# A hybrid attention/RWKV block on one core: key norm at written places, and a reordered end

## The chip, the cores and the metric

The kernel runs on one core of a Trainium2 chip. The metric is the device time of one execution in microseconds (us), as the median of several runs; lower is better. The core has five engines with queues of their own: PE multiplies matrices, DVE and ACT work elementwise (ACT evaluates functions such as Ln and Exp, for which it loads tables), POOL (GpSimd) is a slower elementwise engine, and SP issues most DMAs. Each engine takes its instructions in order; between engines they wait on semaphores.

## The reference

One layer of a trunk with a sequence of 256 tokens and a width of 2048, in float32. A normed input goes through one combined projection; three mixers (stick-breaking attention, forgetting attention, RWKV-7 time mixing) work on it; gated, projected and normed it is added to the input, and a squared-ReLU MLP follows, normed and added as well:

```python
u = rms_norm(x, norm_mix_pre)
proj = u @ w_in
m = g_a * (y_a @ w_branch_a) + g_b * (y_b @ w_branch_b) + g_c * (y_c @ w_branch_c)
x = x + rms_norm(m @ w_out, norm_mix_post)
hdn = square(relu(rms_norm(x, norm_mlp_pre) @ w_mlp_up))
x = x + rms_norm(hdn @ w_mlp_down, norm_mlp_post)
```

In the RWKV part a key vector of each of 16 heads (64 wide) is normed at each token, and a state is carried over the sequence:

```python
kk = kk / maximum(sqrt(sum(kk * kk, axis=-1, keepdims=True)), 1e-12)
sa = einsum('bhvk,bhk->bhv', state, kk_t)
state = state * w_t - sa * (kk_t * a_t) + v_t * k_t      # outer products
y_t = einsum('bhvk,bhk->bhv', state, r_t)
```

## The kernel before, in words

**Matrix products.** All big products run on PE in a split form: a float32 weight chunk of 128x1024 (`raw`) comes by DMA from SP, ACT copies it to a rounded high part `whi` (L152), DVE forms the rest `wlo` (L153), and PE multiplies both with the split activations, adding into the PSUM tiles `gps` (L168, L172 for products with channels on the partitions; L198, L214 for those with tokens there). Three buffers each of `raw`, `whi` and `wlo` rotate, and one chunk is prepared ahead. This stream goes through the whole kernel.

**Mixers beside the stream.** The mixers are Python generators. While the GEMMs are recorded, a model clock advances with each matmul, and a generator is resumed when its due time has come (`yield 3.8`) or when what it names is there (`yield "k3"`). So its small instructions land between the GEMM's in each engine's queue. PE's order in this part is the recorded one (`manual_schedule`); on the other engines a scheduler decides, unless an instruction is pinned with `pin`, which keeps it at its recorded place in its engine's queue.

**The RWKV halves.** `rwkv_half(hf)` handles 8 heads in four pairs `p`, in four chunks of 64 tokens. Each chunk `c` is a chain over the engines: PE adds the state's part (L869, from the state `PB`), ACT and DVE copy it out as `rh` (L873, L874), PE multiplies it with the chunk's triangular inverse (L842 and L882, interleaved), ACT and DVE copy the result into the two tiles `XT` (L886, L887, in turns), PE forms the state's update and the output (L894, L898, L903), DVE updates `PB` (L912, L913 or L915), and ACT copies the output into `g` tiles (L917). After the fourth chunk `gate_norm` starts (L944 to L978, tiles `gn`; its sums are PE's L954).

**Key norm.** `key_norm(hf)` computes the inverse norms of the keys of a half in the tile `b` (by its tag `b6`): four squares on ACT (L635), a split into high (ACT, L646) and low (DVE, L647) of two pairs at a time, sums over a head by PE with a block matrix of ones (L653), a floor (DVE, L655, `sq`), Ln and Exp on ACT with a table load ahead of each (L659, L662), and a Newton step on DVE of five operations a pair of pairs (L667 to L672). `key_norm(0)` runs ahead of the first half's chain. `key_norm(1)`, for the second half, is started as a generator of its own after the first half's first chunk, so that its steps fall beside the chain of the other chunks; the second half reads it much later.

**The end.** The last product (hidden times `w_mlp_down`, the part that is not done in a Strassen-like form above it) goes over four groups `g` of 512 output columns. For each group and token tile `tt` (two of 128 tokens), DVE adds PE's sum to `y` (L1540), ACT squares it with a row sum (L1541), and DVE multiplies it with the gain (L1544). In the last group PE finishes tile 0 first, then tile 1. For each, `rs` comes from DVE (L1139) and a power on POOL (L1140); four final pieces of 512 columns follow on DVE (L1555), each with a store from SP (L1556).

Of the kernel before, what the change touches and what calls it, by code (L numbers as in the profile page):

```python
# [10 lines left out]
F32 = mybir.dt.float32  # L11
F32R = mybir.dt.float32r
# [38 lines left out]
def hybrid_block(ctx, tc, xt, x, gains, params, consts, lora, gup, wst, out):  # L51
# [13 lines left out]
    def nm(s):  # L65
        uid[0] += 1
        return f"{s}_{uid[0]}"
# [4 lines left out]
    def mps():  # L72
        return pm.tile([128, 512], F32, tag="mps", name=nm("mps"), bufs=4)
# [17 lines left out]
    def P(name, i=0, r=slice(0, 128)):  # L91
        return par[r, PC[name] + i:PC[name] + i + 1]
# [535 lines left out]

    def key_norm(hf):
        PR = range(4 * hf, 4 * hf + 4)  # L630
        B6 = rp.tile([128, 6, T], F32, tag="b6", name=nm("b6"), bufs=1)
        rin = [B6[:, i, :] for i in range(4)]
        for i, p in enumerate(PR):
            yield f"k{p}"
            A.activation(rin[i], done[f"k{p}"], AF.Square, scale=P("kk", p))  # L635
        sq = []
        for both in ((0, 1),) if hf == 0 else ((0,), (1,)):
            sqh = []
            for i2 in both:
                s = B6[:, 2 * i2:2 * i2 + 2, :]  # L640
                if hf == 0:
                    hl = [rp.tile([128, 2, T], F32R, tag="BK", name=nm("sqh"), bufs=8) for _ in range(2)]
                else:
                    t = rp.tile([128, 4, T], F32R, tag="Ti", name=nm("sqh"), bufs=1)
                    hl = [t[:, 0:2], t[:, 2:4]]
                A.activation(hl[0], s, AF.Copy)  # L646
                V.tensor_tensor(hl[1], s, hl[0].bitcast(F32), ALU.subtract)  # L647
                sqh.append(hl)
            yield 3.8
            for hl in sqh:  # L650
                ps = mps()
                for n, part in enumerate(hl):
                    PE.matmul(ps.rearrange("p (a b) -> p a b", a=2), bones, part, start=n == 0, stop=n == 1)  # L653
                sq.append(rp.tile([128, 2, T], F32, tag="At", name=nm("sq"), bufs=2))
                V.tensor_scalar(sq[-1], ps.rearrange("p (a b) -> p a b", a=2), 1e-24, None, ALU.max)  # L655
        if hf:
            yield 2.0
        for i2 in range(2):
            A.activation(B6[:, 2 * i2:2 * i2 + 2, :], sq[i2], AF.Ln, scale=float(2.0 ** 20))  # L659
        for i2 in range(2):  # L660
            ri = B6[:, 2 * i2:2 * i2 + 2, :]
            A.activation(ri, ri, AF.Exp, scale=-0.5)  # L662
        yield 4.5
        sc = B6[:, 4:6, :]
        for i2 in range(2):
            ri = B6[:, 2 * i2:2 * i2 + 2, :]
            V.tensor_scalar(ri, ri, 1024.0, None, ALU.mult)  # L667
            V.tensor_tensor(sc, ri, ri, ALU.mult)
            yield 2.0
            V.tensor_tensor(sc, sc, sq[i2], ALU.mult)  # L670
            V.tensor_scalar(sc, sc, -0.5, 1.5, ALU.mult, ALU.add)
            V.tensor_tensor(ri, ri, sc, ALU.mult)  # L672
            yield 3.0
        kin[hf] = rin
        mark(f"kn{hf}")

    def rwkv_half(hf):
# [184 lines left out]
        def duo(ps, hc, d):  # L862
            return ps[hc, 128 * d:128 * d + 128].rearrange("p (a b) -> p a b", a=2)

        for c in range(4):
            if c:
                for i, p in enumerate(PR):
# [17 lines left out]
            for d in range(2):  # L885
                A.activation(XT[d][0:64, :, c, HC[0]], duo(ps, HC[0], d), AF.Copy)  # L886
                V.tensor_copy(XT[d][0:64, :, c, HC[1]], duo(ps, HC[1], d))  # L887
            yield 2.2
            ps = mps()
            psp, psy = ps[:, 0:256], ps[:, 256:512]  # L890
# [9 lines left out]
            if c:  # L900
                for i, p in enumerate(PR):
                    for h, hc in enumerate(HC):
                        PE.matmul(psy[hc, 64 * i:64 * i + 64], PB[:, i, hc], Bt[p][:, c, 64:128], start=False,  # L903
                                  stop=i == 3)
# [624 lines left out]
    for g in range(4):  # L1529
# [7 lines left out]
                    nc.sync.dma_start(out=x1[tt][:, c:c + 1024], in_=xs[tt][:, c:c + 1024])  # L1537
        for tt, ps in enumerate(tok(hp, 3 if g == 3 else 1)):
            yv = ys[tt][:, gs]
            V.tensor_tensor(yv, yv, ps, ALU.add)  # L1540
            A.activation(junk(), yv, AF.Square, accum_out=ss4[:, tt, g:g + 1])  # L1541

            def gained():
                V.tensor_tensor(yv, yv, g4[g], ALU.mult)  # L1544

            if g < 3:
                gained()
                if g == 2:
                    sum4.append(rstd_of(ss4[:, tt, :], eps4[tt], None))
            else:  # L1550
                r4 = rstd_of(ss4[:, tt, :], None, sum4[tt])
                gained()
                for c in range(0, D, 512):
                    cs = slice(c, c + 512)
                    V.scalar_tensor_tensor(x1[tt][:, cs], ys[tt][:, cs], r4, x1[tt][:, cs], ALU.mult, ALU.add)  # L1555
                    nc.sync.dma_start(out=out[tt * 128:tt * 128 + 128, cs], in_=x1[tt][:, cs])  # L1556


# [123 lines left out]
```

## Time and profile before

| what | us |
|---|---|
| median of three runs (lowest, highest) | 1505.39 (1505.01, 1508.8) |
| profiled execution, its own time | 1504.03 |
| its span, first to last instruction | 1502.3 |
| PE busy in the span | 1482.0 |
| DVE busy | 1215.5 |
| ACT busy | 938.5 |
| POOL busy | 91.3 |

Times inside the program are read from the one profiled execution, on a scale that begins with its first instruction. The second to fourth chunk of the first half run from about 408 to 442 us on it, and the end begins at about 1487. A line number is that of the kernel before. In the trace's timeline a row has the start, the length, the engine, the line, the operation, the tiles (out<-in), the shape and how many such instructions in a row it merges; in square brackets stands how long the engine had been idle before it, and what released it.

### The profile page before, as it was taken

To read this page: it belongs to the slowest core of one execution; us is meant where nothing else is said; L and a number is where in the kernel's file an instruction comes from. 1 tells how busy PE (TensorE), PEld (TensorE's weight loads), DVE (VectorE), ACT (ScalarE), POOL (GpSimd) and SP (SyncE) were. 2 spreads that over 40 slices of the span, in tenths; PEclk is the share of its full clock that TensorE was granted. 3 is DMA by queue.
4 is the path that set the end of the run, shared out by engine and by line. 5 is a ranking of instruction groups with operands and counts; after the bars stand their busy time and mean duration, and the time that the engine had idled before them with its cause. 6 is when DMAs were issued, how large, how long until landed. Compare 5 with 4: busy or idle time off the path is not lost.

```text
span 1502.3 us, 22802 instructions
## 1 busy us (share of the span) xinstructions
PE 1482.0 (99%) x8401; PEld 1249.1 (83%) x8401; DVE 1215.5 (81%) x1687; ACT 938.5 (62%) x1398; POOL 91.3 (6%) x160
## 2 busy tenths in 40 slices
PE   9999999999999999999999999999999999999997
PEld 7888888888778888788887888888888888888885
DVE  7666677999769898567646788999899999899986
ACT  7465666664667554575444767777667676677662
POOL 0021000100001100000000000000000000000000
PEclk9999999999999999999999999999999999999998
DMA  7545545545535455445774668888888888888874
GB/s 258 196 150 188 174 169 170 178 164 193 187 116 181 160 181 199 153 147 197 264 281 169 223 207 241 266 241 246 259 263 251 264 255 228 252 259 272 257 247 152
DMA packets 107615, 317.70 MB, mean 211 GB/s; under 512 B 10736, under 2 KB 14704, under 8 KB 107248
## 3 DMA queue, kind: packets, MB, share of 16 engines
q1 hardware_dynamic: 94832, 284.91, 54.9%
q0 software_dynamic: 8064, 29.36, 10.4%
q10 hardware_dynamic: 4608, 1.97, 0.5%
q8 instruction: 66, 1.08, 0.3%
q14 instruction: 45, 0.37, 0.1%
HBM read 282.65 MB, written 4.19 MB: 191 GB/s over the span
## 4 chain that ended last, share of the span: by engine, by line
PE 69%; DVE 1%; issue 1%; POOL 0%; POOLq 0%; ACT 0%; DVEq 0%; ACTq 0%
PE gps L214 20%; PE gps L168 15%; PE gps L172 8%; PE gps L198 5%; PE mps L1412 3%; PE mps L1413 3%; PE mps L1414 3%; PE gps L1414 3%; PE gps L1412 2%; PE gps L1413 2%; PE gps L176 1%; PE mps L767 0%; PE mps L976 0%; DVE wlo L153 0%; PE mps L1103 0%
## 5 line engine op out<-in xcount | busy, mean ns | idle before, releaser
L153 DVE TENSOR_TENSOR wlo<-raw,whi 128x1024 fp32r<-128x1024 f32 x501 | 608.3, 1223 | 162.7 <-ACT whi L152 147.8
L152 ACT ACTIVATE whi<-raw 128x1024 fp32r<-128x1024 f32 x501 | 527.7, 1057 | 260.3 <-PE gps L214 94.1
L168 PE MATMUL gps<-pk,whi 128*128 128x512 f32 x1366 | 346.4, 393 | 0.6 <-ACT whi L152 0.4
L168 PEld LDWEIGHTS gps<-pk,whi 128*128 128x128 f32 x1366 | 253.0, 189 | 50.5 <-ACT whi L152 0.6
L214 PE MATMUL gps<-whi,pk 128*128 128x512 f32 x1144 | 288.5, 392 | 0.0
L214 PEld LDWEIGHTS gps<-whi,pk 128*128 128x128 f32 x1144 | 212.8, 188 | 44.3
L172 PEld LDWEIGHTS gps<-pk,wlo 128*128 128x128 f32 x1456 | 198.5, 190 | 14.4 <-DVE wlo L153 0.5
L172 PE MATMUL gps<-pk,wlo 128*128 128x256 f32 x1456 | 204.1, 282 | 0.0
L214 PE MATMUL gps<-wlo,pk 128*128 128x512 f32 x572 | 156.4, 392 | 0.0
L214 PEld LDWEIGHTS gps<-wlo,pk 128*128 128x128 f32 x572 | 106.3, 188 | 22.4 <-DVE wlo L153 0.3
L1304 ACT ACTIVATE sp<-gps 128x512 f32<-128x512 f32 x52 | 31.1, 598 | 86.2 <-PE gps L176 86.0
L1278 DVE TENSOR_TENSOR sp<-raw,sp 128x1024 fp32r<-128x1024 f32 x67 | 82.0, 1224 | 3.4 <-ACT sp L1277 3.1
L1277 ACT ACTIVATE sp<-raw 128x1024 fp32r<-128x1024 f32 x67 | 70.6, 1054 | 12.8 <-PE mps L1413 4.9
L198 PE MATMUL gps<-whi,pk 128*128 128x512 f32 x264 | 71.0, 391 | 0.0
L1412 PE MATMUL mps<-whi,fm 128*128 128x512 f32 x168 | 66.2, 394 | 0.0
L1413 PE MATMUL mps<-whi,fm 128*128 128x512 f32 x168 | 65.8, 392 | 0.0
L1414 PE MATMUL mps<-wlo,fm 128*128 128x512 f32 x168 | 65.5, 390 | 0.0
L1374 POOL DMA_DIRECT2D raw<-raw x40 | 35.0, 874 | 427.6 <-DVE wlo L153 106.0
L198 PEld LDWEIGHTS gps<-whi,pk 128*128 128x128 f32 x264 | 49.2, 188 | 10.4 <-ACT whi L152 0.2
L1414 PE MATMUL gps<-wlo,fm 128*128 128x512 f32 x126 | 49.2, 391 | 0.5 <-DVE wlo L153 0.5
L1371 DVE TENSOR_TENSOR raw<-raw,raw 128x1024 f32<-128x1024 f32 x40 | 48.9, 1223 | 0.4
L1412 PE MATMUL gps<-whi,fm 128*128 128x512 f32 x126 | 49.2, 391 | 0.0
(378 smaller groups left out, 1962.3 us busy)
## 6 DMA issues: line engine op xcount, KB each, us to landing
raw<-in_wst_dram SPq DMA_DIRECT2D x499, 512.0 KB, 4.3
raw<-raw POOLq DMA_DIRECT2D x40, 512.0 KB, 6.4
sp<-in_wst_dram SPq DMA_DIRECT2D x16, 512.0 KB, 5.3
raw<-sp POOLq DMA_DIRECT2D x8, 512.0 KB, 6.1
sp<-raw POOLq DMA_DIRECT2D x8, 512.0 KB, 6.6
x<-in_x_dram SPq DMA_DIRECT2D x8, 256.0 KB, 5.9
xs<-x SPq DMA_DIRECT2D x2, 1024.0 KB, 3.9
x<-xs SPq DMA_DIRECT2D x4, 512.0 KB, 6.0
```

Source lines behind the costliest of these rows:

```text
L152: A.activation(hi, raw, AF.Copy)
L153: V.tensor_tensor(lo, raw, hi.bitcast(F32), ALU.subtract)
L168: PE.matmul(ps, hi[:, i * 128:i * 128 + 128], pks[i], start=first and i == 0, stop=False)
L172: PE.matmul(ps[:, 0:T], lo[:, i * 128:i * 128 + 128], pks[i][:, 0:T], start=False, stop=False)
L198: PE.matmul(ps[tt], pks[k][:, c:c + 128], w[:, (k - k0) * 512:(k - k0) * 512 + 512], start=k == 0 and part == 0 and w is hl[0], stop=w is ...
L214: PE.matmul(ps[tt], pks[k][:, c:c + 128], w[:, (k - k0) * 512:(k - k0) * 512 + 512], start=k == 0 and part == 0 and w is hl[0], stop=False)
L1277: A.activation(hi, raw, AF.Copy)
L1278: V.tensor_tensor(lo, raw, hi.bitcast(F32), ALU.subtract)
L1371: V.tensor_tensor(x, x, z, ALU.add)
L1412: PE.matmul(Q[f], p, w, start=d == 0 and i == 0, stop=False)
L1413: PE.matmul(Q[f], pl, w, start=False, stop=False)
L1414: PE.matmul(Q[f], p, wl, start=False, stop=d == nd - 1 and i == 1)
```

## The change

The change has two parts. The first is about key norm of the second half. Its generator is no longer started on its own; the first half's chunk loop resumes it at fixed places (`next(beside, None)`): after the XT copies of a chunk and at the end of a chunk. Its yields lose their times, its ACT instructions and the Newton step are pinned, its two Ln stand together and its two Exp, and the Newton step comes behind the fourth chunk. The second part is about the end: the second tile's sum is put ahead of the last two final pieces of the first tile (`issue_after`), one final piece of the second tile is made by ACT (scaling) and GpSimd (adding) and stored from ACT's queue, and the last piece and its store are halved.

```diff
     def key_norm(hf):
+        keep = pin if hf else lambda ins: ins
...
+        def high_low(i2):
...
+            keep(A.activation(hl[0], s, AF.Copy))
+            keep(V.tensor_tensor(hl[1], s, hl[0].bitcast(F32), ALU.subtract))
+            return hl
+
+        def summed(hl):
+            ps = mps()
+            for n, part in enumerate(hl):
+                PE.matmul(ps.rearrange("p (a b) -> p a b", a=2), bones, part, start=n == 0, stop=n == 1)
+            sq.append(rp.tile([128, 2, T], F32, tag="At", name=nm("sq"), bufs=2))
+            V.tensor_scalar(sq[-1], ps.rearrange("p (a b) -> p a b", a=2), 1e-24, None, ALU.max)
...
-        for both in ((0, 1),) if hf == 0 else ((0,), (1,)):
...
+        else:
+            hl = high_low(0)
+            yield
+            summed(hl)
+            hl = high_low(1)
+            yield
+            summed(hl)
+            yield
+        for i2 in range(2):
+            keep(A.activation(B6[:, 2 * i2:2 * i2 + 2, :], sq[i2], AF.Ln, scale=float(2.0 ** 20)))
         if hf:
-            yield 2.0
+            yield
         for i2 in range(2):
             ri = B6[:, 2 * i2:2 * i2 + 2, :]
-            A.activation(ri, ri, AF.Exp, scale=-0.5)
+            keep(A.activation(ri, ri, AF.Exp, scale=-0.5))
         yield 4.5
...
+        beside = iter(()) if hf else key_norm(1)
         for c in range(4):
...
+            if c:
+                next(beside, None)
             yield 2.2
...
-            if c == 0 and hf == 0:
-                start(key_norm(1))
...
+            next(beside, None)
             yield 2.6
+        for _ in beside:
+            pass
         start(gate_norm(hf, y, bon))
...
-            V.tensor_tensor(yv, yv, ps, ALU.add)
+            added = V.tensor_tensor(yv, yv, ps, ALU.add)
...
+            if tt == 0:
+                r4 = rstd_of(ss4[:, 0, :], None, sum4[0])
+                gained()
+                final(0, 512)
+                final(512, 512)
+                r40 = r4
+                continue
+            with tc.issue_after(added.ins):
+                for c in (1024, 1536):
                     cs = slice(c, c + 512)
+                    V.scalar_tensor_tensor(x1[0][:, cs], ys[0][:, cs], r40, x1[0][:, cs], ALU.mult, ALU.add)
+                    nc.sync.dma_start(out=out[0:128, cs], in_=x1[0][:, cs])
+            r4 = rstd_of(ss4[:, 1, :], None, sum4[1])
+            gained()
+            t, cs = junk(), slice(0, 512)
+            A.activation(t, ys[1][:, cs], AF.Copy, scale=r4)
+            G.tensor_tensor(x1[1][:, cs], x1[1][:, cs], t, ALU.add)
+            nc.scalar.dma_start(out=out[128:256, cs], in_=x1[1][:, cs])
+            for c, w in ((512, 512), (1024, 512), (1536, 256), (1792, 256)):
+                final(c, w)
```

The line numbers of the changed kernel are higher by some 15 to 20 from key norm on. Its order at three places follows. First ACT's queue from the third chunk's `rh` copy (L873, in the changed kernel L890) to the split in front of the fourth chunk's: `b` is key norm's tile, `sq` its sums, `XT` the chain's copies, `whi` a weight split, `g` the output copies. Before:

```order
L873 ACTIVATE rh_4330<-mps_4233 64x128 x2
L662 ACT_TABLE_LOAD
L662 ACTIVATE b_773_4166<-b_773_4166 128x512
L152 ACTIVATE whi_4435<-raw_4433 128x1024
L886 ACTIVATE XT_3445<-mps_4357 64x2x64
L886 ACTIVATE XT_3446<-mps_4357 64x2x64
L152 ACTIVATE whi_4469<-raw_4467 128x1024
```

And in the changed kernel:

```order
L890 ACTIVATE rh_4330<-mps_4225 64x128 x2
L152 ACTIVATE whi_4433<-raw_4431 128x1024
L903 ACTIVATE XT_3445<-mps_4353 64x2x64
L903 ACTIVATE XT_3446<-mps_4353 64x2x64
L672 ACT_TABLE_LOAD
L672 ACTIVATE b_773_4166<-sq_4251 128x512
L672 ACTIVATE b_773_4166<-sq_4302 128x512
L152 ACTIVATE whi_4464<-raw_4462 128x1024
L934 ACTIVATE g_754_4073<-mps_4392 128x64
```

The two XT copies stand ahead of the table load, and both Ln come behind them; the second load and the two Exp follow behind the `g` copies, ahead of the fourth chunk's `rh`.

Then DVE's queue at the first half's fourth chunk, from its second XT copy on, where `gn` is the gate norm, `gup` a small weight of it and `wlo` a weight split. Before:

```order
L887 COPY XT_3446<-mps_4479 64x2x64
L153 TENSOR_TENSOR wlo_4585<-raw_4582,whi_4584 128x1024
L948 TENSOR_TENSOR gn_4556<-gn_4557,gn_4555 128x512
L937 TENSOR_TENSOR gup_4645<-gup_4562,gup_4645 128x128
L938 TENSOR_TENSOR gup_4645<-gup_4562,gup_4645 32x128
```

And in the changed kernel:

```order
L904 COPY XT_3446<-mps_4474 64x2x64
L682 TENSOR_SCALAR b_773_4166<-b_773_4166 128x512
L683 TENSOR_TENSOR b_773_4166<-b_773_4166 128x512
L686 TENSOR_TENSOR b_773_4166<-b_773_4166,sq_4251 128x512
L687 TENSOR_SCALAR b_773_4166<-b_773_4166 128x512
L688 TENSOR_TENSOR b_773_4166<-b_773_4166 128x512
L683 TENSOR_TENSOR b_773_4166<-b_773_4166 128x512
L968 TENSOR_TENSOR gn_4556<-gn_4557,gn_4555 128x512
L686 TENSOR_TENSOR b_773_4166<-b_773_4166,sq_4302 128x512
L153 TENSOR_TENSOR wlo_4585<-raw_4582,whi_4584 128x1024
```

Nearly the whole Newton step now lies behind the last XT copy and among the first instructions of the gate norm.

Last, DVE's queue at the end of the program, from the first tile's power on; `x` is the tile of final pieces (2583 the first, 2584 the second). Before:

```order
L1555 SCALAR_TENSOR_TENSOR x_2583_14109<-y_8767,rs_14256,x_2583_14109 128x512 x4
L1540 TENSOR_TENSOR y_8768<-y_8768,gps_14204 128x512
L1139 TENSOR_SCALAR rs_14289<-ss_8074,ssum_14200 128x1
L1544 TENSOR_TENSOR y_8768<-y_8768,pk_13934 128x512
L1555 SCALAR_TENSOR_TENSOR x_2584_14110<-y_8768,rs_14289,x_2584_14110 128x512 x4
```

And in the changed kernel:

```order
L1574 SCALAR_TENSOR_TENSOR x_2583_14109<-y_8767,rs_14256,x_2583_14109 128x512 x2
L1560 TENSOR_TENSOR y_8768<-y_8768,gps_14204 128x512
L1587 SCALAR_TENSOR_TENSOR x_2583_14109<-y_8767,rs_14256,x_2583_14109 128x512 x2
L1159 TENSOR_SCALAR rs_14289<-ss_8074,ssum_14200 128x1
L1564 TENSOR_TENSOR y_8768<-y_8768,pk_13934 128x512
L1574 SCALAR_TENSOR_TENSOR x_2584_14110<-y_8768,rs_14289,x_2584_14110 128x512 x2
L1574 SCALAR_TENSOR_TENSOR x_2584_14110<-y_8768,rs_14289,x_2584_14110 128x256 x2
```

The second tile's sum (L1540, now L1560) has moved ahead of two of the first tile's final pieces, which now stand ahead of the second tile's `rs`.

More of the change, by code (lines that the diff above doesn't have):

```diff
@@ new lines, in key_norm @@
+        sq = []
+        def high_low(i2):
+            s = B6[:, 2 * i2:2 * i2 + 2, :]
+            if hf == 0:
+                hl = [rp.tile([128, 2, T], F32R, tag="BK", name=nm("sqh"), bufs=8) for _ in range(2)]
+            else:
+                t = rp.tile([128, 4, T], F32R, tag="Ti", name=nm("sqh"), bufs=1)
+                hl = [t[:, 0:2], t[:, 2:4]]
+            keep(A.activation(hl[0], s, AF.Copy))
+            keep(V.tensor_tensor(hl[1], s, hl[0].bitcast(F32), ALU.subtract))
+            return hl
@@ new lines, in summed @@
+        def summed(hl):
[4 more added lines that the diff above has]
+            V.tensor_scalar(sq[-1], ps.rearrange("p (a b) -> p a b", a=2), 1e-24, None, ALU.max)
+        for i, p in enumerate(PR):
+            if hf == 0:
+                yield f"k{p}"
+            keep(A.activation(rin[i], done[f"k{p}"], AF.Square, scale=P("kk", p)))
```

50 lines of the change are left out of this document (17 added, 33 removed).

## The prediction

> **What bounds the kernel now.** I read the page first, then PE's waits, then the timeline at the places that the waits name. On the page PE is busy almost all the time:
>
> ```profile
> span 1502.3 us, 22802 instructions
> PE 1482.0 (99%) x8401; PEld 1249.1 (83%) x8401; DVE 1215.5 (81%) x1687; ACT 938.5 (62%) x1398; POOL 91.3 (6%) x160
> ```
>
> So a change that leaves PE's work alone, as this one does, can win only where PE stands still and behind PE's last matmul. PE's waits, longest first (total, times, longest), have these rows for the part that the change touches:
>
> ```profile
> PE mps L894 <- DVE XT L887: 1.6, 3, 1.0
> PE mps L894 <- ACT XT L886: 1.2, 1, 1.2
> ```
>
> L894 is the state product of a chunk of the RWKV recurrence; it reads XT, which ACT and DVE copy out of PSUM. In PE's timeline, the second and the third chunk of the first half, then the same block in the second half, where no key norm runs beside it:
>
> ```profile
> 414.93 0.45 PE L894 MATMUL mps<-XT,Kt 128*64 128x64 f32 x8
> 416.56 0.33 PE L894 MATMUL mps<-XT,Kt 128*64 128x64 f32 x2 [1.18 <-ACT XT L886]
> 418.38 1.20 PE L214 MATMUL gps<-whi,pk 128*128 128x512 f32 x4
> ...
> 427.84 0.33 PE L894 MATMUL mps<-XT,Kt 128*64 128x64 f32 x2
> 430.25 0.39 PE L894 MATMUL mps<-XT,Kt 128*64 128x64 f32 x5 [1.05 <-DVE XT L887]
> 431.56 1.20 PE L214 MATMUL gps<-wlo,pk 128*128 128x512 f32 x4
> ...
> 625.80 0.69 PE L894 MATMUL mps<-XT,Kt 128*64 128x64 f32 x16
> 627.35 1.19 PE L214 MATMUL gps<-whi,pk 128*128 128x512 f32 x4
> ```
>
> From the block's first L894 to the next GEMM matmul it takes 418.38 - 414.93 = 3.45 us and 431.56 - 427.84 = 3.72 us, undisturbed 627.35 - 625.80 = 1.55 us. The two gaps are worth 1.90 + 2.17 = 4.07 us, more than the waits view sums, since the short matmuls between two waits crawl. That is the ceiling of the key norm's part.
>
> Why XT is late: in ACT's queue key norm stands between and ahead of the copies (first rows: second chunk; the others: third).
>
> ```profile
> 414.43 1.28 ACT L662 ACT_TABLE_LOAD   x1
> 416.26 0.25 ACT L886 ACTIVATE XT<-mps 64x128 f32<-64x128 f32 x1
> ...
> 424.47 1.28 ACT L662 ACT_TABLE_LOAD   x1
> 425.77 0.63 ACT L662 ACTIVATE b<-b 128x512 f32<-128x512 f32 x1
> 426.31 1.04 ACT L152 ACTIVATE whi<-raw 128x1024 fp32r<-128x1024 f32 x1
> 427.37 0.27 ACT L886 ACTIVATE XT<-mps 64x128 f32<-64x128 f32 x1
> ```
>
> And in DVE's queue the Newton step of key norm and a weight split push the last copy of the third chunk behind 429.90:
>
> ```profile
> 426.43 0.43 DVE L667 TENSOR_SCALAR b<-b 128x512 f32<-128x512 f32 x1 [1.61 <-ACT b L662]
> 426.89 0.69 DVE L668 TENSOR_TENSOR b<-b 128x512 f32<-128x512 f32 x1
> ...
> 428.77 1.21 DVE L153 TENSOR_TENSOR wlo<-raw,whi 128x1024 fp32r<-128x1024 f32 x1
> 429.90 0.29 DVE L887 COPY XT<-mps 64x128 f32<-64x128 f32 x1
> ...
> 431.66 0.88 DVE L912 TENSOR_TENSOR PB<-mps,PB 64x256 f32<-64x256 f32 x2 [0.87 <-PE mps L903]
> ```
>
> **The key norm, step by step.** It now has fixed places. Second chunk: four squares and one split go in front of the rh copy, in the place of a whi split:
>
> ```profile
> 397.76 1.69 ACT L635 ACTIVATE b<-g,par 128x256 f32<-128x256 f32 x4
> 408.96 0.56 ACT L873 ACTIVATE rh<-mps 64x128 f32<-64x128 f32 x2 [0.85 <-PE mps L869]
> 411.82 0.27 PE L882 MATMUL mps<-rh,SC 64*64 64x64 f32 x1
> ```
>
> The squares (1.69) and the split (0.63, by the Exp row of the same size) replace 1.04, so rh moves by 1.69 + 0.63 - 1.04 = 1.28, of which 0.85 was idle: it starts at about 409.4 and ends at 410.0. PE wants it at 411.82, and about half a us earlier now, since two sum matmuls of key norm move from in front of this block to behind it (four of their shape take 1.10, in the L954 row below). Some 1.3 us are left, so nothing is paid. No key-norm activation stands ahead of the two XT copies now; on DVE they still stand behind two weight splits and, for the second copy, one 0.69 op. I get that copy done about when PE asks for it, cost 0 to 0.3.
>
> Third chunk: the XT copies come ahead of the table load, the two Ln, the second load and the two Exp, and DVE has no Newton step near them. The gap of 2.17 goes. What is late next is the fourth chunk's rh copy, which now waits in ACT's queue behind the Exp. From the end of the third block: PB product 0.88, ACT's four output copies about 0.56 (the rh row, as many elements), load 1.28, two Exp 1.26, whi split 1.04, rh 0.56: 5.6 us. PE's cover is the GEMM work up to the end of this row:
>
> ```profile
> 435.94 1.53 PE L214 MATMUL gps<-whi,pk 128*128 128x512 f32 x6
> ```
>
> 435.94 + 1.53 - 431.56 = 5.9 us. It fits with 0.3 to spare; each us by which the chain is longer is a us of PE. Two of four table loads fall away, 2.57 us of ACT, worth nothing by themselves because PE does not wait there. The Trainium skill speaks against this place: "ScalarE: Activation LUTs", section "What ACT_TABLE_LOAD costs", counts some 2.66 us with a drain for every switch. The trace has the next activation 1.30 us after the load's start (424.47 to 425.77), so the measurement decides; by the page's price the chain would take 1.38 more, PE would wait 1.1, and the gain would shrink by that.
>
> The Newton step (per half 3 x 0.69 + 2 x 0.43 = 2.93, in all 5.86 us of DVE) goes behind the fourth chunk, nearly all behind its last XT copy and in front of the gate norm's second low part, which PE's L954 reads:
>
> ```profile
> 441.02 0.29 DVE L887 COPY XT<-mps 64x128 f32<-64x128 f32 x1
> 444.54 1.23 DVE L153 TENSOR_TENSOR wlo<-raw,whi 128x1024 fp32r<-128x1024 f32 x1 [3.23 <-ACT whi L152]
> 449.39 1.10 PE L954 MATMUL mps<-gn,bones 128*128 128x512 f32 x4
> ```
>
> From 441.31 to 449.39 are 8.1 us, and this distance stays when both move earlier. DVE has to do in it 5.43 of Newton (one 0.43 op goes earlier), two low parts of 0.69 and the split of 1.23: 8.0 us, with 3.23 idle as cover before. L954's second pair comes 0.5 later still. It just fits; I book 0 to 0.4. Together: 4.07 less about 0.25, **3.8 us**; bounds 4.1, and 1.9 if one gap stays. After that PE runs without large waits to the end, so what is won there arrives.
>
> **The end.** DVE's last rows, and PE's last matmuls:
>
> ```profile
> 1490.30 2.74 DVE L1555 SCALAR_TENSOR_TENSOR x<-y,rs,x 128x512 f32<-128x512 f32 x4 [0.46 <-POOL rs L1140]
> 1490.91 0.61 PE L198 MATMUL gps<-wlo,fm 128*128 128x512 f32 x2
> 1492.95 0.68 DVE L1540 TENSOR_TENSOR y<-y,gps 128x512 f32<-128x512 f32 x1
> 1494.48 0.21 DVE L1139 TENSOR_SCALAR rs<-ss,ssum 128x1 f32<-128x1 f32 x1 [0.85 <-ACT junk L1541]
> 1495.73 2.74 DVE L1555 SCALAR_TENSOR_TENSOR x<-y,rs,x 128x512 f32<-128x512 f32 x4 [0.44 <-POOL rs L1140]
> ```
>
> PE is done at 1491.52, but the second tile's sum waits for four final pieces of the first: (1492.95 - 1490.30) / 4 = 0.66 apiece. With two of them moved behind it, it starts at 1490.30 + 1.32 = 1491.62. Its own chain to rs takes 1.53 (1494.48 - 1492.95), but the two moved pieces fill DVE until 1491.62 + 3 x 0.66 = 1493.60, which is later than 1493.15. So rs gains 1494.48 - 1493.60 = 0.88, not 1.33, and the first final piece of the second tile starts at 1493.60 + 1.25 = 1494.85. The two stores moved with the pieces stand in SP's queue where they stood, behind the first two; the new store is the last in ACT's queue, so nothing waits behind it.
>
> Does the shorter rest of the queue count too? Here the DMA rows of one-us stretches decide (last columns: clock, busy share of the 16 engines, GB/s):
>
> ```profile
> 1497.00:1498.00 1.00, 0.00 (x0) 0.00 (x0) 1.00 (x3) 0.00 (x0) 0.00 (x0) 0.50 0.66 256
> 1499.00:1500.00 1.00, 0.00 (x0) 0.00 (x0) 0.00 (x0) 0.00 (x0) 0.00 (x0) 0.50 1.05 322
> 1500.00:1501.00 1.00, 0.00 (x0) 0.00 (x0) 0.00 (x0) 0.00 (x0) 0.00 (x0) 0.50 0.37 131
> ```
>
> The tile's 1 MB moves from about 1497.34 to 1500.37, 3.03 us, with the engines full. So the end is set by when the first piece leaves, and one piece fewer on DVE (0.66) and halved last stores earn next to nothing: the same bytes follow. The traffic starts at 1496.46 and ends at 1499.5, if the GpSimd piece is there in time. Its scaling takes ACT 0.63, then GpSimd adds 128x512; the nearest rows are its 256-wide product and, beside it, a DVE op of that width (min/median/max ns):
>
> ```profile
> L752 POOL TENSOR_TENSOR Bt<-g,ep x8: 686/758/1672, 260.5 to 519.9; 128x256 f32<-128x256 f32 x8
> L740 DVE SCALAR_TENSOR_TENSOR tha<-tha,lw x8: 413/512/919, 263.1 to 521.8; 128x256 f32<-128x256 f32 x8
> ```
>
> Doubled for the width, 1.4 to 3.3 us; I take 1.5, the median doubled. It ends at 1494.85 + 0.63 + 1.5 = 1497.0 (at worst 1498.8) and its packets, some 0.9 later as for the other stores, can start at 1497.9 (1499.7). The other three quarters keep the engines full until 1496.46 + 2.27 = 1498.7. At the median it hides; at worst its own quarter (0.76) ends at 1500.5, and the end gains nothing. So **0.85 us**, bounds 0 and 0.9. The Trainium skill warns of this pairing: "GPSIMD Engine Reference", section "8. Key points", says that GpSimd shares SBUF interfaces with VectorE and collides with its instructions of two SBUF inputs, which the final pieces are. The two rows agree with it: 413 ns grow to 919, 686 to 1672. By it the late end would be the likelier one, with nothing won at the end.
>
> **Sum.** 3.8 + 0.85 = 4.65 us. The profiled execution (span 1502.3, own time 1504.03) would become 1499.4. The median of the runs shown is 1505.39, 1.36 above it; with that difference kept I forecast **1500.7 us**. About 0.3%, 4.5 us, is what a measurement of this kernel can tell from no change: the forecast lies at that bound.
>
> **Rivals.**
> - ACT becomes the bound between the third and the fourth chunk: the 5.6 us chain has only 0.3 to spare. For it: the pinned order lets no whi split or rh pass the Exp. Against: all its durations are measured. One table load as long again or a late PB product takes back 1 to 2.5 us: 1501.7 to 1503.2. Chance 0.12. (By the Trainium skill's price of a switch, named above, it would be 1501.8.)
> - The first gap stays, because its copies on DVE still stand behind two weight splits and wait in turns for ACT: 1.9 less, 1502.6. Against: by my times they end when PE arrives. Chance 0.09.
> - The end wins nothing: GpSimd and DVE slow each other, the GpSimd piece comes last, 0.85 less, 1501.6. For it the 1672 ns row; against, its median of 758. Chance 0.09. (This is the way that the GPSIMD page of the Trainium skill, named above, points to.)
> - Slower: the Newton step holds up the gate norm. Place: DVE between the fourth chunk's last XT copy and L954. Its 5.43 us fit only if the idle 3.23 is usable and the splits don't wait; from the point where the second low part comes after PE's arrival, each us counts. If all 5.43 land on PE, the change costs 5.43 - 4.65 = 0.8: 1506.2. With the end's gain gone as well 1507.0. Against: DVE is in order and its queue there has nothing that waits long. Chance 0.04.
> - It does not do what it says: the order shows the moved instructions, so this is left at nothing.
>
> **Numbers.** The forecast's case (gain 3.9 to 5.0, 1500.4 to 1501.5) has 0.66. Its part with a gain over 4.5 is a bit more than half of it, 0.38; the scatter of medians (the three runs lie from 0.4 below to 3.4 above theirs) carries some of the rivals with a gain near 4 over the bound and I add 0.07: faster 0.45, same 0.51, slower 0.04. The range, with 2 in 10 outside: below, 5.0 and 1 us of scatter, 1499.4; above, the first two rivals, 1503.4.
>
> **What would show it.** Right: the two L894 blocks at some 1.6 us, no wait on XT over 0.4 there; PE 3.8 us earlier at L954's place; the second tile's sum within 0.15 us of PE's end, rs 2 us after it, the stores' traffic about 0.9 earlier against PE's end. Wrong: a PE wait on rh (ACT) in the fourth chunk, on gn (DVE), or GpSimd's add ending later than DVE's last piece with DMA engines idle between.

## The result and the profile of the changed kernel

| | kernel before | changed kernel |
|---|---|---|
| median of ten runs each, same chip (us) | 1504.46 | 1500.82 |
| lowest and highest (us) | 1502.23, 1508.8 | 1499.28, 1502.6 |
| ratio, 95% interval | 1 | 0.9974 (0.9965 to 0.9982) |
| profiled execution: own time, span (us) | 1504.03, 1502.3 | 1500.75, 1499.0 |

The change wins 0.26%, 3.9 us by the ratio (2.7 to 5.3 by the interval); the medians differ by 3.6. The prediction held some 0.3% to be what a measurement of this kernel can tell from no change. The win lies at that bound, where the prediction gave "same" the larger chance (0.51). That it ends so near the 1500.7 of the forecast is partly luck: the kernel before had a median of 1505.39 when the forecast was made, 1504.46 here and 1505.4 to 1505.7 beside the experiments, so a microsecond of such a difference is scatter. The trace says which part won: the key norm all of it, and the end lost half a microsecond.

**The key norm.** The first chunk's state product, which the change leaves alone, is the mark to measure from. (In the kernel before, key norm's four squares and first split run ahead of it, at 397.76 to 402.25; that does not show in its place: it lies at 402.9 to 404.4 in the three kernels with the old key norm and at 403.1 to 404.2 in the others.) Before:

```profile
404.43 0.69 PE L894 MATMUL mps<-XT,Kt 128*64 128x64 f32 x16
```

PE's timeline after, at the first three chunks' products (each with what follows the second and third) and at the gate norm's sum; then the one row of PE's waits that is left in the stretch (total, times, longest):

```profile
403.74 0.69 PE L913 MATMUL mps<-XT,Kt 128*64 128x64 f32 x16
...
414.44 0.69 PE L913 MATMUL mps<-XT,Kt 128*64 128x64 f32 x16
...
415.98 0.73 PE L650 MATMUL mps<-sqh,bones 128*128 128x512 f32 x2
...
425.38 0.69 PE L913 MATMUL mps<-XT,Kt 128*64 128x64 f32 x16
...
426.93 1.19 PE L214 MATMUL gps<-wlo,pk 128*128 128x512 f32 x4
...
444.74 1.10 PE L974 MATMUL mps<-gn,bones 128*128 128x512 f32 x4
```

```profile
PE mps L917 <- DVE XT L904: 0.3, 1, 0.3
```

The second and third block take 415.98 - 414.44 = 1.54 and 426.93 - 425.38 = 1.55 us, as long as the undisturbed one of the second half (1.55), where they took 3.45 and 3.72. From the mark to the gate norm's sum it was 449.39 - 404.43 = 44.96 us and is 444.74 - 403.74 = 41.00: **3.96 us** less. This distance doesn't depend on when the kernel got going, so I compare all experiments on this part by it. It repeats well: 40.98 to 41.05 in the eight kernels with this key norm, 44.97 in e2 below, which has the old one. One trace falls out: e5, with the old key norm too, has 46.44, and there the granted clock of PE was 0.83 between 424 and 434 us, where the kernel before had 1.00.

Two places were said to be tight. ScalarE's queue around the third block, PE's rh product, and VectorE's second low part of the gate norm:

```profile
423.67 0.27 ACT L903 ACTIVATE XT<-mps 64x128 f32<-64x128 f32 x1 [0.36 <-DVE XT L904]
423.96 1.28 ACT L672 ACT_TABLE_LOAD   x1
425.26 1.15 ACT L672 ACTIVATE b<-sq 128x512 f32<-128x512 f32 x2
...
428.60 1.28 ACT L677 ACT_TABLE_LOAD   x1
429.90 1.15 ACT L677 ACTIVATE b<-b 128x512 f32<-128x512 f32 x2
...
431.90 0.56 ACT L890 ACTIVATE rh<-mps 64x128 f32<-64x128 f32 x2
...
432.76 0.68 PE L899 MATMUL mps<-rh,SC 64*64 64x64 f32 x16
...
444.31 0.69 DVE L968 TENSOR_TENSOR gn<-gn,gn 128x512 fp32r<-128x512 f32 x1
```

ScalarE's last XT copy now ends (423.94) when the table load begins. The chain to rh ends at 431.90 + 0.56 = 432.46, 5.53 us after the third block, and PE takes it at 432.76: 0.30 to spare. The low part is done at 445.00; PE asks for it with its second pair, half of 1.10 after 444.74, at 445.29: 0.29 to spare.

**The end.** PE's last matmuls and what follows on VectorE, ScalarE and GpSimd:

```profile
1487.12 0.61 PE L198 MATMUL gps<-wlo,fm 128*128 128x512 f32 x2
...
1487.84 0.68 DVE L1560 TENSOR_TENSOR y<-y,gps 128x512 f32<-128x512 f32 x1
1488.44 1.41 DVE L1587 SCALAR_TENSOR_TENSOR x<-y,rs,x 128x512 f32<-128x512 f32 x2
...
1489.76 0.20 DVE L1159 TENSOR_SCALAR rs<-ss,ssum 128x1 f32<-128x1 f32 x1
...
1491.00 3.21 DVE L1574 SCALAR_TENSOR_TENSOR x<-y,rs,x 128x512 f32<-128x512 f32 x4 [0.44 <-POOL rs L1160]
...
1491.80 1.73 POOL L1593 TENSOR_TENSOR x<-x,junk 128x512 f32<-128x512 f32 x1 [0.83 <-ACT junk L1592]
```

I count from PE's last end, 1491.52 before and 1487.73 now. The sum starts 0.11 after it (1.43 before), the rs operation 2.03 (2.96), the first final piece of the second tile 3.27 (4.21): all as forecast, 0.93 won. Then it goes. VectorE now needs 3.21 us for 1536 columns, where it needed 2.74 for 2048: the piece beside GpSimd's add took 1.48 (the longest on L1574), where a piece alone takes 0.75. In half-microsecond stretches of DMA (last two columns: share of the 16 engines, GB/s) there is a hole where there should be none:

```profile
1493.50:1494.00 0.50, 0.00 (x0) 0.00 (x0) 0.50 (x2) 0.00 (x0) 0.04 (x1) 0.50 1.05 311
1494.00:1494.50 0.50, 0.00 (x0) 0.00 (x0) 0.22 (x1) 0.00 (x0) 0.00 (x0) 0.50 0.29 90
1494.50:1495.00 0.50, 0.00 (x0) 0.00 (x0) 0.00 (x0) 0.00 (x0) 0.00 (x0) 0.50 1.01 389
```

And the program's own last instructions, which the profile books on its last line (minimum/median/maximum ns, then first and last start). Before:

```profile
L1677 POOLq DRAIN  x3: 34/102/5622, 1494.7 to 1502.0; - x3
L1677 SPq DRAIN  x3: 7/7/7, 1501.4 to 1501.7; - x3
L1677 POOLq EVENT_SEMAPHORE  x4: 17/17/17, 1501.5 to 1502.1; - x4
```

And after:

```profile
L1717 POOLq DRAIN  x3: 34/93/6429, 1491.8 to 1498.7; - x3
L1717 SPq DRAIN  x3: 7/7/7, 1497.3 to 1498.5; - x3
L1717 POOLq EVENT_SEMAPHORE  x4: 17/17/17, 1498.2 to 1498.9; - x4
```

A drain is one of the instructions that stand at the end of every engine's program here. SP's first drain starts when all stores have landed, 9.88 us after PE's end before and 9.57 now. GpSimd's long drain is over at 1494.7 + 5.6 = 1500.3 before, a microsecond ahead of SP. After it is over at 1491.8 + 6.4 = 1498.2, 0.9 behind SP, and the span ends 0.8 later. GpSimd's first semaphore step at the end follows the later of the two: it starts at 1501.5 before, right behind SP's drain, and at 1498.2 after, right behind GpSimd's own. Those of ScalarE, VectorE and PE follow at 1501.6 to 1501.7 before and at 1498.4 after. Both drains end 4.6 to 4.7 us after GpSimd's last operation (1494.77 + 0.93 = 1495.70 and 1491.80 + 1.73 = 1493.53). From PE's end to the span's end it was 10.78 us and is now 11.27: the end **loses 0.49**. 3.96 - 0.49 is 3.5; with the 0.7 that PE was earlier at the mark, less the 0.9 that it lost between the gate norm and its last matmul, the spans differ by 3.3.

### The profile page after: what moved, and what is told of

Same layout as the page of the kernel before. It is cut to its first block, busy times and chain, and to the rows that moved or that the text cites. A ratio compares the mean times of both kernels' runs of the same rounds, so it can differ in the third digit from the quotient of the medians.

```text
span 1499.0 us, 22801 instructions
## 1 busy us (share of the span) xinstructions
PE 1480.5 (99%) x8401; PEld 1247.3 (83%) x8401; DVE 1215.2 (81%) x1687; ACT 935.6 (62%) x1397; POOL 93.1 (6%) x161
## 3 DMA queue, kind: packets, MB, share of 16 engines
q0 software_dynamic: 8064, 29.36, 10.4%
## 4 chain that ended last, share of the span: by engine, by line
PE 89%; DVE 3%; issue 3%; DMA 3%; ACT 1%; POOL 1%; SPq 0%; DVEq 0%; POOLq 0%; ACTq 0%
PE gps L214 28%; PE gps L168 21%; PE gps L172 12%; PE gps L198 7%; PE mps L1432 3%; PE mps L1433 3%; PE mps L1434 3%; PE gps L1434 2%; PE gps L1432 2%; PE gps L1433 2%; PE gps L176 1%; DMA raw<-in_wst_dram 1%; DVE wlo L153 1%; DMA x<-in_xt_dram 1%; DMA raw<-raw 1%
## 5 line engine op out<-in xcount | busy, mean ns | idle before, releaser
L198 PEld LDWEIGHTS gps<-whi,pk 128*128 128x128 f32 x264 | 49.2, 188 | 10.4 <-ACT whi L152 0.2
```

The costliest lines, as they stand in the source:

```text
L198: PE.matmul(ps[tt], pks[k][:, c:c + 128], w[:, (k - k0) * 512:(k - k0) * 512 + 512], start=k == 0 and part == 0 and w is hl[0], stop=w is ...
```

## The experiments

PE's end itself scatters: in kernels whose work up to there is the same it lay between 1487.4 and 1491.7, from small waits elsewhere; at the mark of the key norm they already stand 1 us apart (403.1 to 404.2). That is more than the end can win, so the experiments on the end are judged by what follows PE's end. All in us after PE's last matmul; "landed" is SP's first drain. The views give spans and drains to a tenth, so the columns "landed" and "span ends" are good to some 0.05.

| kernel | rs operation | first final piece | landed | span ends | ratio to before (95%) |
|---|---|---|---|---|---|
| before | 2.96 | 4.21 | 9.9 | 10.78 | 1 |
| changed | 2.03 | 3.27 | 9.6 | 11.27 | 0.9974 (0.9965 to 0.9982) |
| e1, key norm alone | 2.96 | 4.21 | 9.9 | 10.70 | 0.9971 (0.9961 to 0.9982) |
| e2, end alone | 2.03 | 3.28 | 9.5 | 11.29 | 1.0006 (0.9997 to 1.0015) |
| e3, no GpSimd | 2.03 | 3.27 | 9.3 | 10.15 | 0.9963 (0.9950 to 0.9976) |
| e4, no GpSimd, whole stores | 2.03 | 3.27 | 9.0 | 9.80 | 0.9963 (0.9950 to 0.9976) |
| e5, before with a late GpSimd op | 2.95 | 4.20 | 10.0 | 12.68 | one run, 1507.23 us |
| e6, GpSimd on the first tile | 2.57 | 3.82 | 9.5 | 10.32 | 0.9970 (0.9959 to 0.9981) |
| e7, one piece between | 1.63 | 3.03 | 8.7 | 9.50 | 0.9959 (0.9946 to 0.9971) |
| e8, small first piece | 1.63 | 3.02 | 8.8 | 9.56 | 0.9970 (0.9959 to 0.9982) |
| e12, as e6, store by SP | 1.79 | 3.03 | 8.8 | 9.56 | 0.9961 (0.9949 to 0.9974) |

**Each half alone.** e1 has the new key norm and the end of before, e2 the reverse.

> Only the key norm's new places; the end as before. I measure the end as the distance from PE's last matmul to the end of the span: 10.78 us before, 11.27 us in the changed kernel. Theory (the key norm wins 3.8 to 3.9 us of PE, the changed end loses 0.5): some 3.9 us faster than before, distance 10.8, so about 0.5 us faster than the changed kernel. Rival (the end wins its 0.85 us as forecast and the key norm only the rest, 2.8 to 3.0): 2.9 us faster than before.

> Only the new end; key norm as before. Theory: rs still comes 0.9 us earlier against PE's end, but the distance from PE's last matmul to the end of the span is 11.2 to 11.4 us instead of 10.78: 0.4 to 0.6 us slower than before. Rival (the changed end gains 0.85 as forecast and the loss seen is scatter): distance 9.9 to 10.0, 0.85 us faster.

In e1 the distance from the mark to the gate norm's sum is 444.63 - 403.64 = 40.99, the end 10.70. In e2 PE's two wait rows on XT read 1.6 and 1.2 us again, as in the kernel before, and the end is that of the changed kernel, 11.29.

The two halves don't touch each other. e1's ratio (4.4 us of gain, 2.7 to 5.9) and the changed kernel's don't differ beyond their intervals, and e2 can't be told from before by time; that it is 0.5 longer rests on the trace.

**The end without GpSimd.** e3 gives the second tile's first piece back to VectorE, e4 makes the last store whole as well:

```diff
-            t, cs = junk(), slice(0, 512)
-            A.activation(t, ys[1][:, cs], AF.Copy, scale=r4)
-            G.tensor_tensor(x1[1][:, cs], x1[1][:, cs], t, ALU.add)
-            nc.scalar.dma_start(out=out[128:256, cs], in_=x1[1][:, cs])
-            for c, w in ((512, 512), (1024, 512), (1536, 256), (1792, 256)):
+            for c, w in ((0, 512), (512, 512), (1024, 512), (1536, 256), (1792, 256)):   # e3
+            for c, w in ((0, 512), (512, 512), (1024, 512), (1536, 512)):                # e4
```

> The changed kernel with the piece of ScalarE and GpSimd back on VectorE: five pieces (three of 512, two of 256 columns), all stores on SP's queue. Theory A (GpSimd's end-of-program drain comes 4.65 us after its last operation and its barrier another 0.8 later, which is what ends the changed kernel): GpSimd's last operation is rs again, its drain ends about 7.9 us after PE's end and nobody waits for it; SP's last landing decides, distance 9.9 to 10.4 us instead of 11.27, 0.9 to 1.4 us faster than the changed kernel. Theory B (the small last stores, 128 KB, land late, and the drain only happens to lie beside them): distance stays at 10.8 to 11.2. Theory C (VectorE slowed by GpSimd is the whole loss): 0.45 us less than the changed kernel, 10.8.

> As the run without GpSimd's piece, and the last piece and its store whole (512 columns, 256 KB) instead of two halves. Theory A: the same as with halves within 0.3 us, distance 9.9 to 10.4, since 1 MB has to move either way. Theory B (small stores land late): 0.4 us or more less than with halves.

VectorE's final pieces of the second tile, and GpSimd's and SP's drains, in e3:

```profile
1490.72 2.87 DVE L1574 SCALAR_TENSOR_TENSOR x<-y,rs,x 128x512 f32<-128x512 f32 x5 [0.44 <-POOL rs L1160]
```

```profile
L1713 POOLq DRAIN  x3: 34/93/5622, 1489.7 to 1497.3; - x3
L1713 SPq DRAIN  x3: 7/7/7, 1496.7 to 1497.0; - x3
```

VectorE does all 2048 columns in 2.87 us, less than the 3.21 for 1536 beside GpSimd. GpSimd's drain is over at 1495.3, 1.4 ahead of SP. Theory A holds: 10.15 of 9.9 to 10.4 expected, where C, a slowed VectorE as the whole loss, had 10.8. The hole in the DMA is gone too: from 1492.5 to 1495.0 no half-microsecond has a share under 0.99. e4 is another 0.35 better, where A allowed up to 0.3 and B wanted at least 0.4. But B's reason, that a small store lands late, isn't borne out. SP's last store in e3 and in e4:

```profile
1493.75 0.41 SPq L1575 DMA_DIRECT2D out_dram<-x  x1
...
1493.44 0.33 SPq L1575 DMA_DIRECT2D out_dram<-x  x1
```

From its start to SP's first drain it is 1496.7 - 1493.75 = 2.95 us with the half and 1496.4 - 1493.44 = 2.96 with the whole store. The half merely starts later, 6.30 us after PE's end instead of 6.04, since VectorE makes five pieces (2.87 us instead of 2.74) and SP issues one store more, the halves at 0.41 instead of 0.33. That is 0.26 of the 0.35; the rest lies within the tenths.

**Is it the drain?** e5 adds one column of GpSimd work to the kernel before:

```diff
+    w = p2.tile([128, 512], F32, tag="junk", name=nm("junk"), bufs=2)
+    G.tensor_tensor(w[:, 0:1], x1[1][:, 2047:2048], cst[:, 2:3], ALU.add)
```

> The kernel before with one more GpSimd operation at the very end, of one column only (128x1, its result unused), which waits for VectorE's last piece (7.0 us after PE's end). Theory A (GpSimd's drain ends some 4.65 us after its last operation, whatever that operation is, and the end of the span some 0.8 later): distance from PE's last matmul to the end of the span 12.5 to 13.4 us instead of 10.78, span 1.7 to 2.6 us longer against PE's end. Rival (the drain is long only behind a big GpSimd operation, or ends at a fixed place): 10.8 to 11.0.

Its row on GpSimd, and the two drains:

```profile
1499.79 0.19 POOL L1558 TENSOR_TENSOR junk<-x,cst 128x1 f32<-128x1 f32 x1 [2.91 <-issue]
```

```profile
L1679 POOLq DRAIN  x3: 34/102/4877, 1499.8 to 1505.2; - x3
L1679 SPq DRAIN  x3: 7/7/7, 1502.7 to 1504.9; - x3
```

The stores land as before (SP at 1502.7), but the drain of an operation of 0.19 us ends at 1504.7, 4.7 after it, and the span at 1505.4, 12.68 after PE's end. So it is the place of GpSimd's last operation that counts, not its size. What the drain waits for the trace doesn't show.

**GpSimd where it isn't last.** e6 keeps e4's second tile and gives the *first* tile's fourth piece to ScalarE and GpSimd, with its store in ScalarE's queue; e12 is the same with the store in SP's queue.

```diff
                 final(512, 512)
+                t, cs = junk(), slice(1536, 2048)
+                A.activation(t, ys[0][:, cs], AF.Copy, scale=r4)
+                G.tensor_tensor(x1[0][:, cs], x1[0][:, cs], t, ALU.add)
+                nc.scalar.dma_start(out=out[0:128, cs], in_=x1[0][:, cs])   # e6; in e12 nc.sync, below
                 r40 = r4
...
-                for c in (1024, 1536):
+                for c in (1024,):
```

> The run without GpSimd's piece and with whole stores, but the FIRST tile's fourth piece by ScalarE and GpSimd, so that only one VectorE piece stands between the second tile's sum and its rs. Theory A (GpSimd costs where its last operation is late; here rs is its last operation): rs 1.64 us after PE's end instead of 2.03, first final piece 2.9 instead of 3.27, distance 9.4 to 9.5 instead of 9.80, GpSimd's drain over by 7.5. Rival (GpSimd beside VectorE slows the sum and the pieces by what it takes off): 9.7 to 9.9.

> The first tile's fourth piece by ScalarE and GpSimd as in the run before, but its store on SP's queue instead of ScalarE's. Theory (there the second tile's square stood behind that store's wait for GpSimd in ScalarE's queue): the square starts right behind the sum, rs 1.85 us after PE's end (VectorE's piece beside GpSimd takes 1.16 instead of 0.75) instead of 2.57, first final piece 3.1 after PE's end, distance from PE's end to the span's end 9.5 to 9.6 instead of 10.32. Rival (GpSimd's work beside VectorE costs it whoever stores): 10.0 or more.

e6 missed both theories: 10.32, where they had 9.4 to 9.5 and 9.7 to 9.9. ScalarE's and VectorE's rows in it:

```profile
1489.08 0.68 DVE L1560 TENSOR_TENSOR y<-y,gps 128x512 f32<-128x512 f32 x1
1489.67 1.16 DVE L1591 SCALAR_TENSOR_TENSOR x<-y,rs,x 128x512 f32<-128x512 f32 x1
...
1490.32 0.38 ACTq L1585 DMA_DIRECT2D out_dram<-x  x1
1490.79 0.63 ACT L1561 ACTIVATE junk<-y 128x512 f32<-128x512 f32 x1 [2.32 <-POOL x L1584]
```

The sum is done at 1489.76, but the square that makes rs from it starts at 1490.79: ahead of it in ScalarE's queue stands the store, which waits for GpSimd's add. With the store on SP the square starts right behind the sum and rs comes at 1.79 (1.85 expected), the end at 9.56 (9.5 to 9.6). VectorE's piece beside GpSimd's add takes 1.16 in both, against 0.75 alone.

**How far can the end go?** e7 has e4's end with only one of the two moved pieces between the sum and rs, the other behind the product with the gain; e8 also splits the second tile's first piece.

```diff
-                for c in (1024, 1536):
+                moved(1024)
             r4 = rstd_of(ss4[:, 1, :], None, sum4[1])
-            gained()
+            with tc.issue_after(gained().ins):
+                moved(1536)
...
+            for c, w in ((0, 256), (256, 256), (512, 512), (1024, 512), (1536, 512)):   # e8
```

> The run without GpSimd's piece and with whole stores, but only one of the two moved pieces between the second tile's sum and rs; the other behind the product with the gain, while GpSimd takes the power. Theory (the end is set by when the second tile's first piece leaves): rs op 1.64 us after PE's end instead of 2.03, the first final piece at 3.05 to 3.1 instead of 3.27, distance 9.6 instead of 9.80. Rival (the end is set by something behind the first piece, VectorE's pieces or the last store's issue at its own pace): 9.8 unchanged.

> As the run with one moved piece between, and the second tile's FIRST piece in two halves (256 columns, 128 KB stores) ahead of three whole ones. Theory (1 MB of traffic behind the first piece sets the end): traffic starts 0.25 to 0.3 us earlier, distance 0.2 to 0.3 less than with a whole first piece. Rival (VectorE's pieces, 0.66 each, and the last store's own 2.5 us to landing set the end): the halves cost VectorE 0.15 more, so the distance is 0.1 to 0.2 longer.

e7, VectorE from the second tile's sum on:

```profile
1490.40 0.68 DVE L1560 TENSOR_TENSOR y<-y,gps 128x512 f32<-128x512 f32 x1
1491.00 0.75 DVE L1586 SCALAR_TENSOR_TENSOR x<-y,rs,x 128x512 f32<-128x512 f32 x1
1491.93 0.21 DVE L1159 TENSOR_SCALAR rs<-ss,ssum 128x1 f32<-128x1 f32 x1 [0.19 <-ACT junk L1561]
...
1492.66 0.75 DVE L1586 SCALAR_TENSOR_TENSOR x<-y,rs,x 128x512 f32<-128x512 f32 x1
1493.33 2.73 DVE L1574 SCALAR_TENSOR_TENSOR x<-y,rs,x 128x512 f32<-128x512 f32 x4
```

The second moved piece fills the time in which GpSimd takes the power; the first final piece starts 3.03 after PE's end and the span ends at 9.50, 0.30 better than e4. The smaller first piece is no use (9.56, the rival's side). e7 has a median of 1498.8 us, 6.2 us (4.4 to 8.1) under before by its ratio. Against the changed kernel the trace gives it an end shorter by 1.77 us; by the times alone the two can't be told apart for certain, since the intervals of their ratios overlap.

**The tight places of the key norm.** e9 moves the logarithm one place later, e10 lets the scheduler place the key norm's instructions at the same due points, e11 makes one Newton product of the second half three times.

```diff
+        if hf:                                                      # e9: ahead of the Ln,
+            yield
         for i2 in range(2):
             keep(A.activation(B6[:, 2 * i2:2 * i2 + 2, :], sq[i2], AF.Ln, scale=float(2.0 ** 20)))
-        if hf:                                                      # e9: not behind it
-            yield
...
-        keep = pin if hf else lambda ins: ins
+        keep = lambda ins: ins                                      # e10
...
-            keep(V.tensor_tensor(sc, ri, ri, ALU.mult))
+            for _ in range(3 if hf and i2 else 1):                  # e11
+                keep(V.tensor_tensor(sc, ri, ri, ALU.mult))
```

> The changed kernel with the key norm's logarithm (table load 1.28, two Ln 1.15) one place later: it stands with the Exp between the third chunk's output copies and the fourth chunk's rh copy, and the weight split that stood there goes behind rh. Theory (ScalarE's chain in front of rh has about 0.3 us to spare): rh comes 1.28 + 1.15 - 1.04 = 1.39 us later than in the changed kernel, so PE waits for it 1.0 to 1.2 us in the fourth chunk, and up to another 1 us for the split behind it: PE's gate-norm sum (L974) 1.0 to 2.2 us later against the chunk before, 1 to 2 us slower than the changed kernel. Rival (PE's cover there is longer than counted): no wait on rh over 0.4, the same time as the changed kernel.

> The changed kernel with the same steps at the same due points, but without holding the key norm's instructions in written order on their engines, so that the scheduler places them: four table loads instead of two, two of them ahead of the third chunk's rh copy; one high part and its low part between the two pairs of XT copies of the second chunk; the Newton step in the third chunk around the XT copies. Theory (it is the place in ScalarE's and VectorE's queues that makes XT and rh late): PE waits on XT or rh come back in the second and third chunk, 2 to 4.5 us in all, and most of the 3.8 us gain is lost. Rival (the due points alone do it): less than 0.5 us of such waits, as fast as the changed kernel.

> The changed kernel with one Newton product of the second half made three times instead of once (the same values again): 2 x 0.69 = 1.38 us more of VectorE between the fourth chunk's last XT copy and the gate norm's second low part. Theory (the 8.1 us there are full and the second low part comes about 0.3 us before PE's second pair asks for it): a PE wait of some 1.1 us on gn at L974, 1.1 us slower than the changed kernel. Rival (VectorE still has idle time there that takes it up): no wait, the same time.

e9, PE's timeline: the fourth chunk's rh product and the gate norm's sum.

```profile
433.39 0.86 PE L899 MATMUL mps<-rh,SC 64*64 64x64 f32 x16 [0.88 <-ACT rh L890]
...
445.78 1.09 PE L974 MATMUL mps<-gn,bones 128*128 128x512 f32 x4
```

PE waits 0.88 for rh; with the mark at 403.44 the distance is 42.34, 1.34 more than in the changed kernel (1.0 to 2.2 expected). Ratio to before 0.9983 (0.9974 to 0.9992).

e10, PE's third block and VectorE beside it:

```profile
425.02 0.33 PE L913 MATMUL mps<-XT,Kt 128*64 128x64 f32 x2
...
426.07 0.63 PE L913 MATMUL mps<-XT,Kt 128*64 128x64 f32 x8 [0.72 <-DVE XT L904]
...
427.41 0.39 PE L913 MATMUL mps<-XT,Kt 128*64 128x64 f32 x5 [0.71 <-DVE XT L904]
...
428.72 1.20 PE L214 MATMUL gps<-wlo,pk 128*128 128x512 f32 x4
...
425.12 0.69 DVE L688 TENSOR_TENSOR b<-b 128x512 f32<-128x512 f32 x1
425.73 0.29 DVE L904 COPY XT<-mps 64x128 f32<-64x128 f32 x1
```

The third chunk's gap is back in full, 428.72 - 425.02 = 3.70 us, and its first copy on VectorE stands right behind the Newton step again. The second chunk's gap is not back. From the mark, 403.39, to the gate norm's sum, 446.55, are 43.16 us: holding the order is worth 2.16 of the 3.96, the new due points 1.80. Theory and rival are each right for one of the two gaps. Ratio 0.9986 (0.9976 to 0.9995).

e11 came out smaller than expected: PE's four sum matmuls take 1.43 instead of 1.10, and no more is lost. VectorE's rows tell why:

```profile
444.49 1.43 PE L975 MATMUL mps<-gn,bones 128*128 128x512 f32 x4
...
444.68 0.69 DVE L969 TENSOR_TENSOR gn<-gn,gn 128x512 fp32r<-128x512 f32 x1
445.29 0.69 DVE L689 TENSOR_TENSOR b<-b 128x512 f32<-128x512 f32 x1
```

The order put the last Newton product (L689) behind the low part, so of the 1.38 us only some 0.69 came in front of it. With the mark at 403.50 the low part is done 445.37 - 403.50 = 41.87 us behind it, where it was 445.00 - 403.74 = 41.26: 0.61 later. Less the 0.29 of slack that is 0.32, and 0.33 was measured. The slack stands; my expectation overlooked that the longer queue is ordered anew. Ratio 0.9972 (0.9962 to 0.9983).

## Why the prediction was right, and where it wasn't

- **The key norm, 3.8 us: right, 3.96 and 3.97 measured** (changed kernel, e1). Both gaps went, the copies no longer stand behind key norm's work, and e10 brought the third chunk's gap back by placement alone. Of the 0.25 that was set aside about 0.1 was paid (4.07 - 3.96). That the win reaches the end of the program, as the prediction says, rests on e1's ratio; in single traces PE's end scatters by as much.
- **rh in the fourth chunk, 5.6 us of chain against 5.9 of cover: right**, 5.53 and 5.83. e9 shows what a longer chain costs. The rival that makes ScalarE the bound there didn't come, nor did the price of a table switch that the Trainium skill gives ("ScalarE: Activation LUTs", section "What ACT_TABLE_LOAD costs"): the first activation behind each load starts 1.30 us after the load (423.96 to 425.26, 428.60 to 429.90), as before.
- **The Newton step "just fits": right**, with 0.29 to spare, so the slower rival was closer than its mechanism looked: 0.69 us more of VectorE work already made PE wait 0.33.
- **rs gains 0.88 and the first final piece with it: right**, 0.93 and 0.94.
- **The end, 0.85 us: wrong, it lost 0.49.** The step that failed is "At the median it hides", said of the GpSimd piece: its cost was looked for in its own store's time and not behind the program. The add itself came nearly as forecast: it was over 5.80 us after PE's end (forecast 1497.0 - 1491.52 = 5.48) and ahead of VectorE's last piece (6.48), so the sign that was named for being wrong, an add that ends later than VectorE, did not come. The runs split the difference between 11.27 and e4's 9.80. GpSimd's drain: the stores of the changed kernel land at 9.57, and by the 0.9 that the span ran on behind SP's drain in the kernel before it would have ended at 10.47; the drain costs 0.8. GpSimd beside VectorE: 10.47 less e3's 10.15, 0.3; the sum had VectorE's pieces as fast as alone. The halved last stores: 10.15 less 9.80, 0.35; the prediction had booked them as earning next to nothing, and they cost. (Each of the three is good to 0.1.) What the reordering of the sum wins is e4's 10.78 - 9.80 = 0.98, so the reasoning from the first piece's start was sound for the part that it described.
- **The rival "the end wins nothing"** named the right place and a fifth of the cause (0.3 of 11.27 - 9.80 = 1.47). GpSimd's add does slow VectorE. The warning of the Trainium skill ("GPSIMD Engine Reference", section "8. Key points") about GpSimd and VectorE instructions with two SBUF inputs is borne out: the piece took 0.66 us off VectorE and put 1.0 on it (3.21 for 1536 columns, where e3 needs 2.87 - 0.66 = 2.21). But more than half of the loss is the drain, which no rival had.
- **The sum.** 4.65 forecast, 3.5 by the two distances, 3.6 by the medians, 3.9 by the ratio. That the forecast time was met to 0.1 us is luck: it was counted from a median of 1505.39, and the kernel before then had 1504.46, which is 0.93 lower and makes up for the 4.65 - 3.64 = 1.01 us of gain that did not come.

## What to carry to other kernels

Ask of every engine when its last operation ends, and what the program still does on it afterwards: a short piece of work on an engine that has little else to do can set the end of the whole span. Work shared out to a second engine is worth only what it leaves the first: measure the first one's pieces beside it, and look at what stands in the queue behind the wait that the sharing adds. An in-order queue that feeds a waiting PE needs its few short copies ahead of anything long, and the order must be held, not hoped for.

## What the runs showed of the hardware

- GpSimd's drain at the end of the program ended 4.6 to 4.7 us after its last operation in all fourteen traces, whether that was a sum of 128x512 (1.73 us), a power of one column (0.93) or a sum of one column (0.19). SP's drains took 7 ns.
- A GpSimd sum of 128x512 in float32 took 1.73 to 1.74 us beside VectorE, and a VectorE final piece beside it 1.16 (e6, e12) or 1.48 (the changed kernel) instead of 0.75.
- A last store of 128 KB had landed 2.95 us after its start, one of 256 KB 2.96 (e3, e4); issuing it took SP 0.41 and 0.33 us.
